# Sums of weight quarters for a Strassen-like product: made in DRAM on one queue, for three more feature tiles, and loaded ready-made

## The chip, the cores and the metric

The kernel runs on one core of a Trainium2 chip. The core has a matrix engine (TensorE; PE in the profile, with its weight loads as PEld), a vector engine (VectorE, DVE), an activation engine (ScalarE, ACT), a general engine (GpSimd, POOL) and a sync engine (SyncE, SP), which in this kernel only issues transfers. Each works through its own list of instructions in order and waits on semaphores; transfers run on 16 DMA engines that all queues share. [...]

The metric is the device time of one execution in microseconds (us): 1148.0 us before the change, the median of three runs (1146.92 to 1148.77).

## The reference

One layer on a sequence of 1024 tokens and a width of 1024, all in float32:

```python
h = x
hn = rmsnorm(h, norm_mix_g)
z = hn @ w_in                                    # pooling columns, then q, k, v of 8 heads
a = pool_mixer(u, pool_w, pool_b, pool_scale)    # trailing means over 2, 4, 8, 16 tokens
o = chunk_attention(q, k, v, rel_bias)           # own chunk of 64 and 8 before, bias per head
h = h + concat([a, o]) @ w_out
hn = rmsnorm(h, norm_ffn_g)
gt, val = split(hn @ w_up)                       # 2 x 2816 columns: "the first projection"
gt = causal_dwconv(gt, conv_w, conv_b)
h = h + (gelu(gt) * val) @ w_down                # "the second projection"
gate = sigmoid(rmsnorm(h, norm_ple_g) @ w_ple_gate + b_ple_gate)
h = h + gate * (p @ w_ple)
return rmsnorm(h, final_g)
```

## The kernel before

Every float32 factor is split into a high and a low part in the matrix engine's format (`split`, L133 to L135: ACT makes the high part at L134, DVE the low part at L135), and each product is three matmuls (`mm3`, L127 to L131). The order of PE's work is written out by hand. The other engines' instructions are put into their lists by a scheduler, which goes by the program's order and by priorities; what the code marks with `keep_in_program_order` stays in the program's order on its queue.

**Stages by time.** To 44 us the first loads, to 284 us attention together with the input projections and the pooling, to 345 us the output projection begins, to about 800 us the rest of it and the first projection, to 1040 us the second projection, then the gate and the end.

**Attention** (the loop over i, L566 to L601) has 64 iterations: 8 heads of 8 token tiles. An iteration computes the scores of tile i (`scores`: PE at L341, L342 or L349, L350, then DVE at L343 or L351, which also adds the head's bias, then ACT's exponential at L353), transposes the probabilities of tile i - 2 (`probs_t`: PE L367, evicted by ACT L374 and DVE L375), and, every second iteration, multiplies two tiles' probabilities with the values (`values(w)`, w = (i - 5) / 2, PE L384 and L385); its output is written to `o32` by DVE at L391. PE's time in between is filled with matmuls of the input projections, whose weights SP loads at L181 into two buffers.

**The bias.** At the first tile of head h, `load_bias(h + 1)` loads the next head's bias (SP, L320) into the buffer that head h - 1 used, so the transfer is issued when that head's last scores are done. ACT negates it (L321), and POOL masks two corners (L322, L323). ACT meets L321 early in the head and stands there until the load has landed; the bias itself is needed a head later.

**The Strassen-like products.** Both projections into and out of the 2816 features use seven products of 2x2 blocks in place of eight. A weight tile has four quarters a11, a12, a21, a22, and the products need a11, a12, a22 and four sums: s1 = a21 + a22 (product 5), s2 = s1 + a11 (6), s4 = s2 + a12 (3), s3 = a21 + a11 (7).

- For the second projection, the sums of its 11 weight tiles k are made in DRAM (`SD`) during attention: `weight_sums(k, part)` in six parts, two iterations apart, with a new k every four iterations from i = 8. SP makes the plain copies (L547: s1 = a21, s3 = a21, s2 = s1, s4 = s2), POOL the accumulates (L550). A part waits for the transfer of the part before it, on whichever queue it stands.
- For the first projection, a feature tile fi from 3 on gets its four quarters by plain loads (L735, SP), and POOL sums them in SBUF (L744). For fi = 0, 1 and 2 (`by_load`) the sums are made by the transfers themselves: `fetch` loads a quarter on SP (L735) and adds a second one with an accumulate of POOL (L737) for products 5 and 7; products 6 and 3 take the buffer of product 5, to which `prepare` adds one more quarter (POOL, L772) after the split of the former value. That is 15 plain loads and 12 accumulates of 256 KB.

`prepare(upto)` splits the weights of the steps up to four ahead of PE, and `fetch` asks for loads up to two steps ahead of that. There are five buffers (`rawu`). `step(fi, n)` runs product n and evicts it; `keep` (L829, L830) is the eviction by ACT that the next product on the same PSUM bank waits for.

**The pooling.** POOL computes the trailing means of groups 2 and 3 (L455 to L469) when their projections are done, late in attention.

## Time and profile before

| what | value |
|---|---|
| runs | 1148.77, 1146.92, 1148.0 us; median 1148.0 us |
| profiled execution | 1149.12 us, its span 1147.3 us |
| PE busy, 0 to 44 us | 40.97 of 44 us |
| 44 to 284 us (attention) | 235.65 of 240 us, DMA share 0.59 |
| 284 to 345 us | 61.00 of 61 us |
| 345 to 800 us (to the end of the first projection) | 452.08 of 455 us, DMA share 0.27 |
| 800 to 1040 us (second projection) | 238.47 of 240 us, DMA share 0.48 |
| 1040 to 1147 us | 97.06 of 107 us |

The profile is one execution; its times are counted from the start of its span. A busy PE is one with a matmul in flight: neighbours overlap, so a stretch can read 100% and still hold the same matmuls in more or less time. A row of the timeline gives start, duration, engine, line, operation, count and, in brackets, the idle time before it with what ended it. "SPq" is SP's list of issues; a transfer's landing is counted from its issue. Where an engine's idle time is put down to a matmul or to an operation that was long done, the wait was for something else, often a transfer.

### The profile page before, as it was taken

Reading aid. Unit: us, or ns where it says so; the run is one execution under the profiler, and the core shown is the slowest. Engines: PE = TensorE matmul, PEld = TensorE weight load, DVE = VectorE, ACT = ScalarE, POOL = GpSimd, SP = SyncE. Lnnn points to the kernel's source line nnn. Section 1 sums busy time; section 2 is a strip of 40 time slices with the busy share of each in tenths; the row PEclk is TensorE's granted clock in tenths of the full one; section 3 lists DMA queues with packets and bytes.
Section 4 is the critical chain, followed back from the end, with each engine's and each line's share of the span. In section 5 each row is a group of like instructions: output and inputs, shape, how many; then the busy total and the mean of one; then the engine's idle time right before and its main releaser. Section 6 shows DMA issues by size and latency. Waiting matters only on the chain.

```text
span 1147.3 us, 15673 instructions
## 1 busy us (share of the span) xinstructions
PE 1125.2 (98%) x5697; PEld 954.8 (83%) x5697; DVE 894.4 (78%) x1396; ACT 582.9 (51%) x1019; POOL 247.4 (22%) x224
## 2 busy tenths in 40 slices
PE   8999989999999999999999999999999999999996
PEld 7988988888888787888888888888788888888996
DVE  7678877878756787998989998898896779774553
ACT  8568677765654544434343434343444557563342
POOL 0012222165003212434343434343000000000000
PEclk9999999999999999999999999999999999999998
DMA  7236788633611163221323131323673564310111
GB/s 264 74 101 143 178 206 187 157 65 123 207 19 28 32 151 100 67 100 66 101 65 110 59 102 61 111 62 121 222 275 101 165 205 162 102 47 1 40 60 49
DMA packets 62701, 128.76 MB, mean 112 GB/s; under 512 B 7360, under 2 KB 9664, under 8 KB 62272
## 3 DMA queue, kind: packets, MB, share of 16 engines
q1 hardware_dynamic: 54416, 113.02, 30.1%
q0 software_dynamic: 8064, 14.68, 8.2%
q8 instruction: 44, 0.72, 0.3%
q14 instruction: 33, 0.27, 0.1%
q10 hardware_dynamic: 144, 0.07, 0.0%
HBM read 112.01 MB, written 38.80 MB: 131 GB/s over the span
## 4 chain that ended last, share of the span: by engine, by line
PE 87%; DVE 4%; issue 3%; DMA 3%; ACT 2%; SPq 0%; DVEq 0%; POOLq 0%; POOL 0%; ACTq 0%
PE PS L129 27%; PE PS L131 27%; PE PS L130 27%; PE PS L367 2%; PE PS L384 1%; PE PS L385 1%; DMA F<-in_w_down 1%; DVE R L135 1%; DVE B L375 1%; DMA F<-in_bias 1%; PE PS L342 1%; PE PS L341 1%; DVE F L343 1%; DMA F<-in_w_qk 1%; ACT F L353 0%
## 5 line engine op out<-in xcount | busy, mean ns | idle before, releaser
L129 PE MATMUL PS<-R,R 128*128 128x512 f32 (+1 forms) x944 | 361.8, 383 | 3.0 <-ACT V L830 1.8
L131 PE MATMUL PS<-R,R 128*128 128x512 f32 (+1 forms) x944 | 358.5, 380 | 0.0
L130 PE MATMUL PS<-R,R 128*128 128x512 f32 (+1 forms) x880 | 340.5, 387 | 0.3 <-DVE R L230 0.3
L135 DVE TENSOR_TENSOR R<-F,R 128x512 fp32r<-128x512 f32 (+1 forms) x214 | 193.5, 911 | 28.5 <-ACT R L134 28.0
L134 ACT ACTIVATE R<-F 128x512 fp32r<-128x512 f32 (+1 forms) x218 | 132.4, 621 | 150.1 <-PE PS L130 83.3
L129 PEld LDWEIGHTS PS<-R,R 128*128 128x128 f32 x944 | 177.7, 188 | 34.9 <-ACT V L830 2.2
L131 PEld LDWEIGHTS PS<-R,R 128*128 128x128 f32 x944 | 177.7, 188 | 33.9 <-DVE R L135 0.4
L130 PEld LDWEIGHTS PS<-R,R 128*128 128x128 f32 x880 | 165.7, 188 | 32.6 <-DVE R L230 1.6
L744 POOL TENSOR_TENSOR F<-F 128x512 f32<-128x512 f32 x76 | 142.7, 1878 | 222.5 <-DVE R L135 142.0
L130 PE MATMUL PS<-B 128*128 128x512 f32 x316 | 123.3, 390 | 1.5 <-DVE B L135 1.5
L129 PE MATMUL PS<-B 128*128 128x512 f32 x316 | 123.4, 390 | 0.0
L131 PE MATMUL PS<-B 128*128 128x512 f32 x316 | 123.1, 390 | 0.0
L134 ACT ACTIVATE B<-F 128x512 fp32r<-128x512 f32 (+1 forms) x86 | 55.8, 649 | 83.3 <-PE PS L130 59.0
L135 DVE TENSOR_TENSOR B<-F,B 128x512 fp32r<-128x512 f32 (+1 forms) x86 | 61.4, 715 | 29.1 <-ACT B L134 28.6
L654 POOL TENSOR_TENSOR small<-small 128x4 f32<-128x4 f32 (+1 forms) x7 | 7.7, 1095 | 338.5 <-DVE small L653 338.5
L130 PE MATMUL PS<-B,R 128*128 128x256 f32 x256 | 72.3, 283 | 0.0
L130 PEld LDWEIGHTS PS<-B 128*128 128x128 f32 x316 | 59.3, 188 | 14.6 <-DVE B L135 2.3
L129 PEld LDWEIGHTS PS<-B 128*128 128x128 f32 x316 | 59.3, 188 | 12.6 <-ACT B L134 0.3
L131 PEld LDWEIGHTS PS<-B 128*128 128x128 f32 x316 | 59.3, 188 | 12.3
L353 ACT ACTIVATE F<-F,small 128x640 f32<-128x640 f32 (+2 forms) x64 | 44.4, 694 | 20.8 <-DVE small L351 12.8
L129 PE MATMUL PS<-B,R 128*128 128x256 f32 x192 | 54.8, 285 | 0.0
L131 PE MATMUL PS<-B,R 128*128 128x256 f32 x192 | 54.5, 284 | 0.0
(163 smaller groups left out, 1934.6 us busy)
## 6 DMA issues: line engine op xcount, KB each, us to landing
F<-in_w_up SPq DMA_DIRECT2D x91, 256.0 KB, 2.8
SD<-in_w_down POOLq DMA_DIRECT2D x44, 256.0 KB, 6.3
GD<-F SPq DMA_DIRECT2D x22, 512.0 KB, 2.6
R<-GD SPq DMA_DIRECT2D x44, 256.0 KB, 5.3
F<-SD SPq DMA_DIRECT2D x44, 256.0 KB, 2.7
F<-in_w_down SPq DMA_DIRECT2D x33, 256.0 KB, 3.5
SD<-in_w_down SPq DMA_DIRECT2D x22, 256.0 KB, 5.3
SD<-SD SPq DMA_DIRECT2D x22, 256.0 KB, 5.0
```

What stands on the lines that cost most here:

```text
L129: pe.matmul(ps, ahi, bhi, start=first, stop=False, skip_group_check=more)
L130: pe.matmul(ps, ahi, blo, start=False, stop=False, skip_group_check=more)
L131: pe.matmul(ps, alo, bhi, start=False, stop=last, skip_group_check=more)
L134: act.activation(hi, src, AF.Copy)
L135: dve.tensor_tensor(lo, src, rv(hi), ALU.subtract)
L341: pe.matmul(PS[:, 4 + z, 0:320], q, K2[:, ks], start=True, stop=False)
L342: pe.matmul(PS[:, 4 + z, 0:320], q, K1[:, ks], start=False, stop=True)
L343: dve.tensor_tensor_reduce(S.rearrange("p (a b) -> p a b", a=2), PS[:, 4:6, 0:320], b.rearrange("p (a b) -> p a b", a=2), 1.0, BIG, ALU.ad ...
L353: act.activation(S[:, 0:n], S[:, 0:n], AF.Exp, bias=s_[:, 0:1], scale=-1.0, accum_out=s_[:, 1:2])
L367: pe.transpose(pst[:, j * P:(j + 1) * P], S[:, j * P:(j + 1) * P], ident)
L375: dve.tensor_tensor(lo, pst, rv(hi), ALU.subtract)
L744: pool.tensor_tensor(rawu[to], rawu[a], rawu[b], op)
```

## The change

The sums move altogether to POOL's queue. `weight_sums` now makes the plain copies there too, and it makes the sums of 14 weight tiles: those of the first projection's feature tiles 0, 1 and 2 come first (`UP_SUMS` = 3), then the 11 of the second projection. A new tile starts every three iterations from i = 7. In each iteration in which parts are due, `sums_due` first lets POOL copy one column of `o32`, the attention output w = (i - 6) // 2, into an unused column of `small`; so the transfers behind it in POOL's list start only when that output has been written. The up projection's tiles 0, 1 and 2 then load their seven factors ready-made, one plain load each on SP, 21 in all; their accumulates are gone.

```diff
+        UP_SUMS = 3
+        SD = [dr.tile([NF // 2 + UP_SUMS, P, 512], F32, name=f"SD{n}") for n in range(4)]
...
-            def copy(t, src):
-                tc.keep_in_program_order(sp.dma_start(t, src))
-            def grow(t, i, j):
-                tc.keep_in_program_order(pool.dma_start(t, weight(k, i, j), accum_op=ALU.add))
-            if part == 0:
-                copy(s1, weight(k, 2, 1))
-                copy(s3, weight(k, 2, 1))
-            elif part == 1:
-                grow(s1, 2, 2)
-                grow(s3, 1, 1)
...
+        def weight_sums(u, part):
+            s1, s2, s4, s3 = [t[u] for t in SD]
+            a11, a12, a21, a22 = [quarter(u, (i, j)) if u < UP_SUMS else weight(u - UP_SUMS, i + 1, j + 1)
+                                  for i in range(2) for j in range(2)]
+            todo = {0: ((s1, a21, None), (s3, a21, None)), 1: ((s1, a22, ALU.add), (s3, a11, ALU.add)),
+                    2: ((s2, s1, None),), 3: ((s2, a11, ALU.add),), 4: ((s4, s2, None),), 5: ((s4, a12, ALU.add),)}
+            for to, src, op in todo[part]:
+                tc.keep_in_program_order(pool.dma_start(to, src, **({"accum_op": op} if op else {})))
+        def sums_due(i, wi):
+            due = [divmod(i - 7 - 2 * part, 3) + (part,) for part in range(6)]
+            due = [(u, part) for u, z, part in due if z == 0 and 0 <= u < NK + UP_SUMS]
+            if due:
+                h, w = wi // 4, wi % 4
+                a = slice(HD * (h % 2), HD * (h % 2) + HD)
+                tc.keep_in_program_order(pool.tensor_copy(small[a, 78:79], o32[a, h // 2, w * 256:w * 256 + 1]))
+            for u, part in due:
+                weight_sums(u, part)
...
-            for part in range(6):
-                k, z = divmod(i - 8 - 2 * part, 4)
-                if z == 0 and 0 <= k < NK:
-                    weight_sums(k, part)
+            if i >= 7:
+                sums_due(i, (i - 6) // 2)
...
-                sp.dma_start(rawu[i], quarter(fi, qs[0]))
-                for q in qs[1:]:
-                    pool.dma_start(rawu[i], quarter(fi, q), accum_op=ALU.add)
-                held[owner, qs[0]] = i
+                if fi in by_load:
+                    src = SD[SUM_OF[q]][fi] if q in SUM_OF else quarter(fi, plain[q])
+                else:
+                    src = quarter(fi, q)
+                sp.dma_start(rawu[i], src)
+                held[owner, q] = i
...
-                if fi in by_load and n in grows:
-                    pool.dma_start(rawu[t], quarter(fi, grows[n]), accum_op=ALU.add)
```

How this stands in the engines' lists, at three places. In the rows, SD0 to SD3 are s1, s2, s4 and s3, F and small are SBUF tiles, and the names behind "waits" are semaphores: DMAHW of SP's transfers, DMASW of POOL's, the others of engines. Line numbers of the changed kernel are one or two off those of before.

SP's list around the bias load that was issued at 154.75 us, before:

```order
L181 DMA F_70<-in_w_in 128x1024 [waits DMAHW7_49,DVE_49,Activation_49]
L547 DMA SD1_77<-SD0_76 16x4096 [waits DMAHW0_49,DMASW5_49]
L547 DMA SD0_76<-in_w_down 128x512 [waits DMAHW1_49]
L547 DMA SD2_78<-SD1_77 16x4096 [waits DMAHW2_49,DMASW7_49]
L547 DMA SD0_76<-in_w_down 128x512 [waits DMAHW3_49]
L547 DMA SD3_79<-in_w_down 128x512 [waits DMAHW4_49]
L547 DMA SD1_77<-SD0_76 16x4096 [waits DMAHW5_49,DMASW1_49]
L547 DMA SD3_79<-in_w_down 128x512 [waits DMAHW6_49]
L547 DMA SD2_78<-SD1_77 16x4096 [waits DMAHW7_49,DMASW3_49]
L181 DMA F_70<-in_w_in 128x1024 [waits DMAHW0_49,DVE_49,Activation_49]
L547 DMA SD0_76<-in_w_down 128x512 [waits DMAHW1_49]
L320 DMA F_70<-in_bias 128x640 [waits DMAHW3_49,DVE_49,Pool_49]
```

and now, from the bias load before it to the one after:

```order
L321 DMA F_70<-in_bias 128x640 [waits DMAHW3_49,DVE_49,Pool_49]
L182 DMA F_70<-in_w_in 128x1024 [waits DMAHW7_49,DVE_49,Activation_49]
L182 DMA F_70<-in_w_in 128x1024 [waits DMAHW1_49,DVE_49,Activation_49]
L321 DMA F_70<-in_bias 128x640 [waits DVE_49,Pool_49]
L182 DMA F_70<-in_w_in 128x1024 [waits DMAHW4_49,DVE_49,Activation_49]
L182 DMA F_70<-in_w_in 128x1024 [waits DMAHW5_49,DMAHW0_49,DVE_49]
L321 DMA F_70<-in_bias 128x640 [waits DVE_49,Pool_49]
```

The sums have left SP's list, and with them SP's waits for POOL's transfers (DMASW) ahead of weight and bias loads.

POOL's list in a head of attention, before:

```order
L322 MEMSET F_70 64x64 [waits DVE_49,Activation_49]
L323 MEMSET F_70 64x64 [waits Pool_49]
L550 DMA SD0_76<-in_w_down 128x512 [waits DMAHW3_49,DMASW5_49]
L550 DMA SD3_79<-in_w_down 128x512 [waits DMAHW4_49,DMASW6_49]
L550 DMA SD1_77<-in_w_down 128x512 [waits DMAHW5_49,DMASW7_49]
L550 DMA SD2_78<-in_w_down 128x512 [waits DMAHW7_49,DMASW0_49]
L550 DMA SD0_76<-in_w_down 128x512 [waits DMAHW4_49,DMASW1_49]
```

and now, around the masks of one head:

```order
L563 COPY small_73<-F_70 64x1 [waits DVE_49,Pool_49]
L554 DMA SD0_76<-in_w_down 128x512 [waits DMASW0_49]
L554 DMA SD3_79<-in_w_down 128x512
L554 DMA SD1_77<-in_w_up 128x512 [waits DMASW4_49]
L323 MEMSET F_70 64x64 [waits Activation_49]
L324 MEMSET F_70 64x64
L563 COPY small_73<-F_70 64x1 [waits Pool_49]
L554 DMA SD1_77<-SD0_76 16x4096 [waits DMASW5_49]
L554 DMA SD2_78<-in_w_up 128x512 [waits DMASW7_49]
```

Each group of transfers now stands behind a copy that waits for an attention output, the plain copies stand among the accumulates, and the masks stand behind the first groups of their head instead of ahead of all.

POOL's list where the first projection begins, before:

```order
L654 TENSOR_TENSOR small_73<-small_73 128x4 [waits DVE_49]
L772 DMA F_70<-in_w_up 128x512 [waits DMASW7_49,DMASW0_49,DVE_49]
L737 DMA F_70<-in_w_up 128x512 [waits DMAHW2_49,DMASW1_49,DVE_49]
L772 DMA F_70<-in_w_up 128x512 [waits DMASW6_49,DMASW2_49,DVE_49]
L772 DMA F_70<-in_w_up 128x512 [waits DMASW3_49,DMASW2_49,DVE_49]
L737 DMA F_70<-in_w_up 128x512 [waits DMAHW7_49,DMASW4_49,DVE_49]
L737 DMA F_70<-in_w_up 128x512 [waits DMAHW0_49,DVE_49]
L772 DMA F_70<-in_w_up 128x512 [waits DMASW4_49,DVE_49]
L772 DMA F_70<-in_w_up 128x512 [waits DMASW6_49,DVE_49]
L744 TENSOR_TENSOR F_70<-F_70 128x512 [waits DMAHW6_49,DMAHW4_49,DVE_49]
```

and now:

```order
L812 TENSOR_TENSOR TB_3184<-TB_3184 128x512 [waits DVE_49]
L653 TENSOR_TENSOR small_73<-small_73 128x4 [waits DVE_49]
L741 TENSOR_TENSOR F_70<-F_70 128x512 [waits DMAHW4_49,DMAHW6_49,DMAHW0_49,DVE_49]
L741 TENSOR_TENSOR F_70<-F_70 128x512 [waits DMAHW5_49,DMAHW2_49,DVE_49]
L741 TENSOR_TENSOR F_70<-F_70 128x512 [waits DMAHW1_49,Pool_49]
```

The accumulates in place are gone; POOL's next work is the sums in SBUF for feature tile 3.

More of the change, by code (lines that the diff above doesn't have):

```diff
@@ L106, in trunk @@
         GD = dr.tile([NF, P, SEQ], F32, name="GD")
-        SD = [dr.tile([NF // 2, P, 512], F32, name=f"SD{n}") for n in range(4)]
+        UP_SUMS = 3
+        SD = [dr.tile([NF // 2 + UP_SUMS, P, 512], F32, name=f"SD{n}") for n in range(4)]
         b_pool = tc.tile_pool(name="b1", bufs=1)
@@ L540, in weight, with quarter @@
             return w_down[k + NK * (j - 1), :, (i - 1) * 512:i * 512]
-        def weight_sums(k, part):
-            s1, s2, s4, s3 = [t[k] for t in SD]
-            def copy(t, src):
-                tc.keep_in_program_order(sp.dma_start(t, src))
-            def grow(t, i, j):
-                tc.keep_in_program_order(pool.dma_start(t, weight(k, i, j), accum_op=ALU.add))
-            if part == 0:
-                copy(s1, weight(k, 2, 1))
-                copy(s3, weight(k, 2, 1))
-            elif part == 1:
-                grow(s1, 2, 2)
-                grow(s3, 1, 1)
-            elif part == 2:
-                copy(s2, s1)
-            elif part == 3:
-                grow(s2, 1, 1)
-            elif part == 4:
-                copy(s4, s2)
-            else:
-                grow(s4, 1, 2)
+        def quarter(fi, q):
+            return w_up[fi, q[0], :, q[1] * 512:(q[1] + 1) * 512]
+        def weight_sums(u, part):
[15 more added lines that the diff above has]
+                weight_sums(u, part)
         load_bias(0)
         for i in range(NI + 3):
-            for part in range(6):
-                k, z = divmod(i - 8 - 2 * part, 4)
-                if z == 0 and 0 <= k < NK:
-                    weight_sums(k, part)
+            if i >= 7:
+                sums_due(i, (i - 6) // 2)
             if i < NI:
@@ L707, in trunk @@
         order = ahead + [(fi, n) for fi in range(NF) for n in steps[fi]]
-        by_load = (0, 1, 2)
-        chains = {1: ((0, 0),), 5: ((1, 0), (1, 1)), 2: ((0, 1),), 7: ((1, 0), (0, 0)), 4: ((1, 1),)}
-        grows = {5: (0, 0), 6: (0, 1)}
+        by_load = range(UP_SUMS)
+        plain = {1: (0, 0), 2: (0, 1), 4: (1, 1)}
+        SUM_OF = {5: 0, 6: 1, 3: 2, 7: 3}
         loads = []
@@ L715, in trunk @@
             if fi in by_load:
-                if n in chains:
-                    loads.append((i, (fi, n), chains[n]))
+                loads.append((i, (fi, n), n))
             else:
                 need = {1: ((0, 0),), 5: ((1, 0), (1, 1)), 2: ((0, 1),), 6: ((0, 0),), 3: ((0, 1),), 7: (), 4: ()}[n]
-                loads += [(i, fi, (q,)) for q in need if not any(l[1:] == (fi, (q,)) for l in loads)]
+                loads += [(i, fi, q) for q in need if not any(l[1:] == (fi, q) for l in loads)]
         prepared, fetched, done = [0], [0], [0]
@@ L727, in fetch @@
             while fetched[0] < len(loads) and not used[fetched[0] % len(rawu)]:
-                place, owner, qs = loads[fetched[0]]
+                place, owner, q = loads[fetched[0]]
                 fi = owner if isinstance(owner, int) else owner[0]
@@ L734, in fetch @@
                 used[i] = True
-                sp.dma_start(rawu[i], quarter(fi, qs[0]))
-                for q in qs[1:]:
-                    pool.dma_start(rawu[i], quarter(fi, q), accum_op=ALU.add)
-                held[owner, qs[0]] = i
-        def quarter(fi, q):
-            return w_up[fi, q[0], :, q[1] * 512:(q[1] + 1) * 512]
+                if fi in by_load:
[4 more added lines that the diff above has]
+                held[owner, q] = i
         def summed(to, a, b, op=ALU.add):
@@ L753, in prepare @@
                 if fi in by_load:
-                    m = n if n in chains else 5
-                    t = held[(fi, m), chains[m][0]]
-                    done_with = [] if n in grows else [t]
+                    t = held[(fi, n), n]
+                    done_with = [t]
                 else:
@@ L922, in weight_sum @@
         def weight_sum(n, k):
-            return SD[{5: 0, 6: 1, 3: 2, 7: 3}[n]][k]
+            return SD[SUM_OF[n]][UP_SUMS + k]
         def T(k):
```

## The prediction

> **What bounds the kernel now.** The page comes first: TensorE (PE) is busy for 98% of the span.

> ```profile
> span 1147.3 us, 15673 instructions
> PE 1125.2 (98%) x5697; PEld 954.8 (83%) x5697; DVE 894.4 (78%) x1396; ACT 582.9 (51%) x1019; POOL 247.4 (22%) x224
> ...
> q0 software_dynamic: 8064, 14.68, 8.2%
> ```

> The change adds no matrix product and takes none away, so only PE's idle time and new stalls can move the end. Next, the busy time in three stretches (us from the start, then length, busy time of PE, PEld, DVE, ACT, POOL, granted clock, DMA share, GB/s): attention, the first projection's first features, and a stretch of its later ones.

> ```profile
> 94.00:236.00 142.00, 137.65 (x893) 122.72 (x893) 113.44 (x276) 103.92 (x223) 32.28 (x48) 1.00 0.74 169
> 370.00:460.00 90.00, 87.08 (x392) 71.51 (x391) 69.57 (x91) 41.51 (x66) 21.19 (x19) 1.00 0.38 93
> 460.00:520.00 60.00, 60.00 (x266) 49.69 (x266) 54.47 (x57) 24.71 (x35) 23.79 (x13) 1.00 0.24 81
> ```

> PE idles 142.00 - 137.65 = 4.35 us in the first and 2.92 us in the second. These 7.3 us, 0.6% of the span, are all that the change can win. The waits of PE name the causes (total us, times, longest):

> ```profile
> PE PS L367 <- DVE B L375: 4.2, 3, 2.9
> PE PS L129 <- ACT V L830: 1.8, 1, 1.8
> ...
> PE PS L129 <- ACT F L830: 1.2, 1, 1.2
> ```

> **Part 1, the first projection.** The timeline (start us, us, engine, line, operation, count, idle before it) of both L830 waits, then the landings of L772's transfers and of SP's plain loads:

> ```profile
> 393.72 0.93 POOL L772 DMA_DIRECT2D F<-in_w_up  x1 [0.95 <-DVE R L135]
> 397.88 1.15 ACT L134 ACTIVATE R<-F 128x512 fp32r<-128x512 f32 x2 [5.30 <-PE PS L131]
> 399.56 0.50 PE L129 MATMUL PS<-R,R 128*128 128x512 f32 x1 [1.75 <-ACT V L830]
> ...
> 429.81 0.63 ACT L134 ACTIVATE R<-F 128x512 fp32r<-128x512 f32 x1 [3.50 <-PE PS L131]
> 430.98 0.50 PE L129 MATMUL PS<-R 128*128 128x512 f32 x1 [1.17 <-ACT F L830]
> ```

> ```profile
> DMA to landing us min/median/max: 3.9/4.1/4.6
> ...
> F<-in_w_up SPq DMA_DIRECT2D x91, 256.0 KB, 2.8
> ```

> An accumulate may start only when the split of the buffer's former value is done, and it lands 4.1 us later (393.72 + 4.1 = 397.8). ACT stands at the next split (5.30 and 3.50 us), and the eviction L830 that PE needs stands behind that. The change takes out all 12 accumulates and makes 21 plain loads out of 15. Each is asked for three steps ahead and waits only for a free buffer. Three steps are 36 matmuls of 60.00 / 266 = 0.23 us, 8.1 us; a load that lands in 2.8 us, or in twice that, is hidden. Six more issues on SP, each below the 0.52 us of the issues shown further down, lie beside some 60 us of products: nothing, and without that cover 3 us. Gain: 1.75 + 1.17 = **2.9 us**, bounded by 0 (another wait right behind) and by 3.5 (each gap also costs the overlap of two matmuls, 0.50 - 0.23). I take 2.9, since the third stretch, where nothing accumulates in place, shows no gap.

> **Part 2, the sums on POOL.** In attention 88 transfers for 11 sums become 112 for 14, all on POOL. Rows of the DMA line, of POOL's pooling and of the attention outputs 0, 23 and 25:

> ```profile
> L550 POOL DMA_DIRECT2D SD<-in_w_down x44 | 37.3, 962 | 42.2 <-issue 30.2 <-DMA SD<-SD 8.9 <-DVE R L277 1.8
> ```

> ```profile
> 236.74 2.69 POOL L455 TENSOR_TENSOR F<-F 128x271 f32<-128x271 f32 x3 [15.88 <-DVE small L354]
> ```

> ```profile
> 72.36 0.41 DVE L391 TENSOR_TENSOR F<-PS,F 64x256 f32<-64x256 f32 x1
> ...
> 231.68 0.43 DVE L391 TENSOR_TENSOR F<-PS,F 64x256 f32<-64x256 f32 x1
> ...
> 243.83 0.41 DVE L391 TENSOR_TENSOR F<-PS,F 64x256 f32<-64x256 f32 x1
> ```

> Output 0 releases the first transfers, output 25 the last: 171 us for 112 issues of 0.96 us. The DMA engines are fuller than POOL. q0 carried 56 accumulates, 0.082 x 1147 / 56 = 1.68 us of all 16 engines for each; the first stretch has a DMA share of 0.74, and if all of that were sums, 14/11 gives 0.94. The queue nearly fills but holds. POOL may fall some us behind in the middle; from iteration 46 on no sum starts, and it recovers. Behind it wait the bias masks L322, which have a head's length, and the pooling of groups 2 and 3: output 23 releases the last transfers ahead of it at 232 us, 5 us before it starts, and POOL had idled 15.88 us for it. The 50 one-column copies have no row; from nothing up to the 0.96 us of an issue for each they add at most 48 us to 112 x 0.96 = 108 us of issues in 171, so even that fits. Nearest are POOL's masks of 64x64, 0.18 us, some 9 us in all; hidden, I take nothing.

> ```profile
> L323 POOL MEMSET F<- 64x64 f32 x8 | 1.5, 182 | 0.4
> ```

> **Part 3, the bias loads.** PE's longest wait is a bias load's. SP's issues, then ACT, then PE, in the order of the wait:

> ```profile
> 102.65 0.33 SPq L320 DMA_DIRECT2D F<-in_bias  x1
> ...
> 152.92 0.52 SPq L181 DMA_DIRECT2D F<-in_w_in  x1
> 153.50 1.14 SPq L547 DMA_DIRECT2D SD<-in_w_down  x2
> 154.75 0.52 SPq L320 DMA_DIRECT2D F<-in_bias  x1
> ```

> ```profile
> 105.83 0.74 ACT L321 ACTIVATE F<-F 128x640 f32<-128x640 f32 x1
> ...
> 131.64 0.74 ACT L321 ACTIVATE F<-F 128x640 f32<-128x640 f32 x1 [0.75 <-DMA F<-in_bias]
> ...
> 161.30 0.74 ACT L321 ACTIVATE F<-F 128x640 f32<-128x640 f32 x1 [2.34 <-DMA F<-in_bias]
> ...
> 188.38 0.74 ACT L321 ACTIVATE F<-F 128x640 f32<-128x640 f32 x1 [1.46 <-DMA F<-in_bias]
> ```

> ```profile
> 163.54 0.77 PE L367 MATMUL PS<-ident,F 128*128 128x128 f32 x5 [2.87 <-DVE B L375]
> ```

> ```profile
> DMA to landing us min/median/max: 3.0/3.2/6.5
> ```

> ```profile
> SPq L547 <- DMA SD<-in_w_down: 105.0, 22, 10.3
> ```

> The load of 154.75 us had a 512 KB weight load and two plain copies ahead of it on SP's queue, took 6.5 us, and ACT waited 2.34 us at L321, PE 2.87. SP itself had stood at L547 (105 us in all). With the sums off SP the weight load can go earlier, the copies are gone, and at 4.4 us of landing the bias is there at 159 us, just as ACT asks (161.30 - 2.34). Gain 2.87 us.

> There is a price. Before, the masks stood in POOL's order ahead of the next accumulates, so the accumulates paused around each bias load. Now they run through it: output 4, which releases some, comes 3.5 us before the issue at 102.65. How long a bias load then takes, no row shows. The nearest is a weight load amid accumulates, at 134.31 us, against the best of its kind:

> ```profile
> F<-in_w_in SPq DMA_DIRECT2D x1, 512.0 KB, 5.7
> ```

> ```profile
> DMA to landing us min/median/max: 3.5/4.2/7.3
> ```

> ```profile
> 99.14 0.43 DVE L391 TENSOR_TENSOR F<-PS,F 64x256 f32<-64x256 f32 x1
> ```

> ```profile
> 108.01 0.82 DVE L375 TENSOR_TENSOR B<-PS,B 128x640 fp32r<-128x640 f32 x1
> ```

> ```profile
> 108.89 0.77 PE L367 MATMUL PS<-ident,F 128*128 128x128 f32 x5
> ```

> Those 2.2 us are for 512 KB; a bias of 320 KB takes 5/8 of it, 1.4: landing L = 4.4 us, bounds 3.0 (nothing added) and 7.3 (the longest of this queue). The load at 102.65 had 3.2 us until ACT asked, and PE had no slack behind it (108.89 against 108.83); the one behind 131.64 was already waited for at about 3.1. So these two turns lose L - 3.2 = 1.2 and L - 3.1 = 1.3 us. The turn at 161.30 wins 2.87 up to L = 4.8 (it issues 0.6 us sooner, without the two copies); that at 188.38, whose load took 4.2, stays. Sum of attention: 1.2 + 1.3 - 2.9 = **-0.4 us**; -4.1 at 3.0 and +11 at 7.3.

> [...]

> **Sum.** -2.9 - 0.4 = -3.3 us. The profiled execution took 1149.1 us, 1.8 of it around its span, and becomes 1145.8; the median of 1148.0 lies 1.1 below it, so the forecast is **1144.7 us**, 0.29% faster. About 0.2%, 2.3 us, is what a measurement of this kernel can tell from no change.

> **The rivals.** (a) The bias loads hardly feel the accumulates (L = 3.0): attention wins 4.1, the sum is -7.0, 1141.0. For it: only the 6.5 us load had much ahead of it. Against: a DMA share near 0.9.

> (b) *Slower*: the accumulates never pause and the bias loads are late at every head. With the four turns above the sum is 4L - 21 us: nothing at L = 5.3, slower by more than 0.2% from L = 5.9, and at 6.5, the longest seen for a bias, +5, 1153. For it: one load did take 6.5, and a weight load 7.3. Against: both had transfers of their own queue ahead, which now leave it.

> (c) It doesn't do what it says: the gaps at 399.56 and 430.98 close, but the next split or eviction holds PE there (DVE is busy 69.57 of 90 us), or L near 5.2 takes the gain back: within 0.2%, about 1148. Against: the later features, with as many splits and a busier DVE, show no gap.

> (d) The copies or a full DMA ring make POOL late by more than the 5 us before the pooling; the mixer's splits follow, and PE waits some 5 us net, 1153. Against: the 15.88 us of idle there.

> **Chances.** Forecast with its neighbours (1143.5 to 1145.7) 0.35, (a) 0.20, (c) 0.26, (b) 0.15, (d) 0.04. Faster 0.55, same 0.26, slower 0.19. Leaving out a tenth on either side, the range is 1140.8 to 1152.5; the faster cases alone fill 1140.8 to 1145.7.

> **What would show it.** Right: no L830 wait of PE before 460 us, no gap of over 1 us near 160 us, waits of ACT at L321 of 1 to 2 us at several heads, a DMA share near 0.9 from 94 to 236 us. Wrong: bias landings of 6 us or more, waits of PE at L367 of over 2 us at several heads, or a pooling that starts after 245 us.

## The result, and the profile after

| | before | after |
|---|---|---|
| median of seven runs on one chip | 1148.77 us | 1158.74 us |
| lowest and highest | 1146.65, 1153.72 us | 1156.72, 1169.40 us |
| ratio | | 1.0091, 95% interval 1.0069 to 1.0114 |

The change makes the kernel 10 us slower, beyond the 0.2% that can be told from nothing and beyond the range on record. The profiled execution of after is the longest of the seven (1169.4 us), so its losses are larger than the usual ones; e1's profile below, of an execution of usual length, shows losses of the same kind.

The page of after, to be held against the first fence of the prediction:

```profile
span 1167.6 us, 15724 instructions
PE 1133.2 (97%) x5697; PEld 963.6 (83%) x5697; DVE 893.8 (77%) x1396; ACT 583.1 (50%) x1019; POOL 287.5 (25%) x328
```

The three stretches of before, in after (length, busy time of PE, PEld, DVE, ACT, POOL, granted clock, DMA share, GB/s):

```profile
94.00:236.00 142.00, 125.67 (x786) 113.46 (x785) 98.79 (x238) 89.44 (x191) 75.45 (x140) 0.94 0.90 206
370.00:460.00 90.00, 90.00 (x410) 74.76 (x410) 66.02 (x92) 45.44 (x74) 15.50 (x11) 1.00 0.22 71
460.00:520.00 60.00, 60.00 (x267) 49.67 (x266) 52.67 (x57) 23.68 (x34) 21.61 (x12) 1.00 0.26 84
```

The second row is part 1 as forecast: the 2.92 us of idle time are gone. The first row is the loss: 16.33 us of idle time where 4.35 stood, a clock of 0.94, and a DMA share of 0.90.

ACT's wait for the five bias loads issued between 90 and 250 us (total us, times; before: 4.6, 3), their landing (before: 3.0/3.3/6.5), and then ACT's rows behind them:

```profile
  ACT F L322: 22.1, 5
...
DMA to landing us min/median/max: 6.7/7.8/8.2
```

```profile
109.71 0.74 ACT L322 ACTIVATE F<-F 128x640 f32<-128x640 f32 x1 [3.59 <-DMA F<-in_bias]
140.55 0.74 ACT L322 ACTIVATE F<-F 128x640 f32<-128x640 f32 x1 [5.89 <-DMA F<-in_bias]
172.58 0.74 ACT L322 ACTIVATE F<-F 128x640 f32<-128x640 f32 x1 [2.86 <-DMA F<-in_bias]
205.11 0.74 ACT L322 ACTIVATE F<-F 128x640 f32<-128x640 f32 x1 [5.41 <-DMA F<-in_bias]
238.08 0.74 ACT L322 ACTIVATE F<-F 128x640 f32<-128x640 f32 x1 [4.38 <-DMA F<-in_bias]
```

and PE's gaps, one behind each of them, in the timeline of PE:

```profile
112.66 0.76 PE L368 MATMUL PS<-ident,F 128*128 128x128 f32 x5 [3.56 <-DVE B L376]
142.51 0.58 PE L131 MATMUL PS<-B,R 128*128 128x256 f32 x1 [4.38 <-DVE B L136]
174.82 0.77 PE L368 MATMUL PS<-ident,F 128*128 128x128 f32 x5 [3.41 <-DVE B L376]
207.49 1.33 PE L368 MATMUL PS<-ident,F 128*128 128x128 f32 x5 [4.87 <-DVE B L376]
245.42 1.33 PE L368 MATMUL PS<-ident,F 128*128 128x128 f32 x5 [4.07 <-DVE B L376]
```

Read the two together: every late bias holds ACT for 3 to 6 us, and 2 to 3 us after ACT's negation has begun (at the last turn 7, with 5 us of held-up work of ACT in between) PE comes out of a gap of 3.4 to 4.9 us, 20.3 us in all. PE's rows name DVE, but DVE had waited 3.53, 3.29 and 5.92 us for ACT's part of the same eviction (L375) at three of them, and 4.46 us for ACT's exponential (L354) ahead of the split at 142.51; both stand behind L322 in ACT's list.

A second loss shows in the granted clock. The 8 us behind four of the gaps, in pieces of 4 us (length, busy time of PE, clock, DMA share, GB/s):

```profile
142.51:146.51 4.00, 4.00 (x18) 0.50 1.00 209
146.51:150.51 4.00, 4.00 (x29) 0.78 1.04 367
...
207.49:211.49 4.00, 4.00 (x16) 0.50 0.95 172
211.49:215.49 4.00, 4.00 (x19) 0.79 0.26 46
245.42:249.42 4.00, 4.00 (x16) 0.50 0.07 29
249.42:253.42 4.00, 4.00 (x20) 0.84 0.02 4
```

Behind three of the gaps PE runs at half clock for 5 to 6 us: each of these stretches loses about 4 x 0.50 + 4 x 0.2 = 2.8 us, and the one behind 174.82 some 1.7 (0.60 and 0.98); behind 112.66 the clock stays at 1.00. The sum for this execution: idle time from 94 to 284 us 20.8 instead of 4.35 (+16.4), half clock +10.0, part 1 -2.9, and 1.5 us less idle time between 460 and 840 us: +22, beside 1167.6 - 1147.3 = 20.3 seen. It closes to 2 us.

### The profile page after: what moved, and what is told of

Same layout as the page of the kernel before. It is cut to its first block, busy times and chain, and to the rows that moved or that the text cites. A ratio compares the mean times of both kernels' runs of the same rounds, so it can differ in the third digit from the quotient of the medians.

```text
span 1167.6 us, 15724 instructions
## 1 busy us (share of the span) xinstructions
PE 1133.2 (97%) x5697; PEld 963.6 (83%) x5697; DVE 893.8 (77%) x1396; ACT 583.1 (50%) x1019; POOL 287.5 (25%) x328
## 4 chain that ended last, share of the span: by engine, by line
PE 87%; DMA 5%; issue 3%; DVE 2%; ACT 2%; POOL 0%; SPq 0%; DVEq 0%; POOLq 0%; ACTq 0%
PE PS L131 27%; PE PS L132 27%; PE PS L130 27%; DMA F<-in_bias 3%; PE PS L368 2%; PE PS L385 1%; PE PS L386 1%; DVE B L376 1%; DVE F L344 1%; DMA F<-in_w_qk 1%; PE PS L343 1%; DMA SD<-SD 1%; PE PS L342 1%; DMA R<-GD 0%; ACT F L354 0%
## 5 line engine op out<-in xcount | busy, mean ns | idle before, releaser
L131 PE MATMUL PS<-R,R 128*128 128x512 f32 (+1 forms) x880 | 341.0, 387 | 0.4 <-DVE R L231 0.3
L136 DVE TENSOR_TENSOR R<-F,R 128x512 fp32r<-128x512 f32 (+1 forms) x214 | 191.5, 901 | 19.4 <-ACT R L135 18.8
L135 ACT ACTIVATE R<-F 128x512 fp32r<-128x512 f32 (+1 forms) x218 | 132.9, 620 | 144.5 <-PE PS L131 86.6
L131 PEld LDWEIGHTS PS<-R,R 128*128 128x128 f32 x880 | 166.0, 189 | 32.5 <-DVE R L231 1.4
L131 PE MATMUL PS<-B 128*128 128x512 f32 x316 | 123.1, 390 | 0.2 <-DVE B L136 0.2
L135 ACT ACTIVATE B<-F 128x512 fp32r<-128x512 f32 (+1 forms) x86 | 55.7, 648 | 79.8 <-PE PS L131 54.5
L136 DVE TENSOR_TENSOR B<-F,B 128x512 fp32r<-128x512 f32 (+1 forms) x86 | 61.2, 713 | 27.7 <-ACT B L135 27.4
L131 PE MATMUL PS<-B,R 128*128 128x256 f32 x256 | 73.0, 285 | 4.4 <-DVE B L136 4.4
L131 PEld LDWEIGHTS PS<-B 128*128 128x128 f32 x316 | 59.3, 188 | 13.1 <-DVE B L136 0.6
L130 PEld LDWEIGHTS PS<-B 128*128 128x128 f32 x316 | 59.3, 188 | 12.2
L554 POOL DMA_DIRECT2D SD<-in_w_down x66 | 52.9, 845 | 36.1 <-issue 24.5
L376 DVE TENSOR_TENSOR B<-PS,B 128x640 fp32r<-128x640 f32 (+2 forms) x64 | 42.0, 656 | 21.2 <-ACT B L375 20.5
L354 ACT ACTIVATE F<-F,small 128x640 f32<-128x640 f32 (+2 forms) x64 | 44.3, 693 | 21.0 <-DVE small L352 12.9
## 6 DMA issues: line engine op xcount, KB each, us to landing
F<-in_w_up SPq DMA_DIRECT2D x85, 256.0 KB, 2.8
SD<-in_w_down POOLq DMA_DIRECT2D x66, 256.0 KB, 5.9
F<-SD SPq DMA_DIRECT2D x56, 256.0 KB, 2.7
GD<-F SPq DMA_DIRECT2D x22, 512.0 KB, 2.6
R<-GD SPq DMA_DIRECT2D x44, 256.0 KB, 5.4
F<-in_w_down SPq DMA_DIRECT2D x33, 256.0 KB, 3.2
SD<-SD POOLq DMA_DIRECT2D x28, 256.0 KB, 5.9
F<-in_w_in SPq DMA_DIRECT2D x10, 512.0 KB, 5.9
```

The source lines that it names most:

```text
L130: pe.matmul(ps, ahi, bhi, start=first, stop=False, skip_group_check=more)
L131: pe.matmul(ps, ahi, blo, start=False, stop=False, skip_group_check=more)
L135: act.activation(hi, src, AF.Copy)
L136: dve.tensor_tensor(lo, src, rv(hi), ALU.subtract)
L354: act.activation(S[:, 0:n], S[:, 0:n], AF.Exp, bias=s_[:, 0:1], scale=-1.0, accum_out=s_[:, 1:2])
L376: dve.tensor_tensor(lo, pst, rv(hi), ALU.subtract)
```

## The experiments

Medians are from runs beside the kernel before on the same chip; the ratio is to that kernel.

| run | median, us | ratio (95%) | idle PE, 94 to 284 us |
|---|---|---|---|
| before (with e1 to e4; e5 to e8; e9 to e11) | 1148.9; 1149.4; 1149.0 | | 4.35 |
| after | 1158.7 | 1.0091 (1.0069 to 1.0114) | 20.8 |
| e4 no sums in attention | 1138.6 | 0.9903 (0.9875 to 0.9930) | 1.1 |
| e1 negation moved in the text only | 1161.1 | 1.0098 (1.0065 to 1.0131) | 13.9 |
| e5 negation late | 1146.9 | 0.9980 (0.9968 to 0.9992) | 3.9 |
| e8 before, negation late | 1144.9 | 0.9969 (0.9957 to 0.9980) | 1.3 |
| e2 before, copies on POOL | 1154.1 | 1.0046 (1.0028 to 1.0063) | 5.7 |
| e3 after, copies on SP | 1185.7 | 1.0310 (1.0285 to 1.0336) | 38.8 |
| e6 after without gates | 1155.4 | 1.0059 (1.0035 to 1.0083) | 15.1 |
| e7 13 sums, pace 4 | 1167.3 | 1.0164 (1.0147 to 1.0181) | 12.2 |
| e9 e5 without gates | 1145.6 | 0.9964 (0.9943 to 0.9985) | 1.6 |
| e10 e9 with 13 sums | 1140.9 | 0.9926 (0.9902 to 0.9950) | 1.2 |
| e11 e5 with copies on SP | 1139.0 | 0.9915 (0.9893 to 0.9938) | 1.3 |

**Is it the transfers at all? e4.**

```diff
-                weight_sums(u, part)
+                if part < 0:
+                    weight_sums(u, part)
...
-                    src = SD[SUM_OF[q]][fi] if q in SUM_OF else quarter(fi, plain[q])
+                    src = quarter(fi, plain.get(q, (1, 0)))
...
-            return SD[SUM_OF[n]][UP_SUMS + k]
+            return weight(k, 1, 1)
```

> The changed kernel without any transfer of the sums in attention (the one-column copies stay); where a sum would be loaded, a plain weight tile of the same size is, so the output is not the reference's. Every theory in which those transfers cost expects bias landings of 2.5 to 3.2 us, no PE idle of over 2 us in attention, granted clock 0.995 or more and 1141 to 1145. If the one-column copies, the other loads or the chip's clock are to blame, the time stays above 1150.

Measured 1138.6 us, a little under the expectation. The stretch of attention, and the row of the bias loads among the DMA issues (count, size, median landing):

```profile
94.00:284.00 190.00, 188.88 (x1186) 167.38 (x1185) 155.58 (x365) 132.37 (x278) 44.74 (x102) 1.00 0.17 54
```

```profile
F<-in_bias SPq DMA_DIRECT2D x8, 320.0 KB, 2.9
```

So the sums' transfers cost 20 us in after, and 10 in before, whose twelve accumulates in place are also gone here. The one-column copies, which stay in e4, cost nothing that shows (PE idles 1.1 us in the stretch).

**Is it ACT's stand? e1, e5, e8.** e1 put the negation of the bias five tiles later in the program:

```diff
-            act.activation(b, b, AF.Copy, scale=-1.0)
+        def negate_bias(h):
+            b = biasb[h % 2]
+            act.activation(b, b, AF.Copy, scale=-1.0)
...
+                if t == 4 and h + 1 < N_HEADS:
+                    negate_bias(h + 1)
```

> The changed kernel, with the negation of each head's bias (ACT) and its two masks (POOL) moved from the load to the fifth tile of the head before, some 13 us behind the load; the first head keeps its place. Theory A (ACT standing in order at the negation behind a load of 7 to 8 us is what costs): no wait of ACT at the negation over 1 us although the loads still land after 6 us or more, PE waits at L368's line (the identity product that opens a score's transposes) under 4 us in sum instead of 16.3, granted clock back at 0.99 or more, time 1143 to 1148. Rival B (the full DMA rings as such, through late weight loads and starved splits): a gain of under 4 us, time 1154 to 1159, PE idle elsewhere in attention.

Measured 1161.1 us. The edit didn't do what it says: the scheduler gave the negation the same places in ACT's list from the second head on, so it still stands right behind the load, and the run is nearly a repeat of after, in an execution of usual length:

```profile
107.48 0.74 ACT L324 ACTIVATE F<-F 128x640 f32<-128x640 f32 x1 [3.11 <-DMA F<-in_bias]
...
197.02 0.74 ACT L324 ACTIVATE F<-F 128x640 f32<-128x640 f32 x1 [4.76 <-DMA F<-in_bias]
```

It says nothing for or against either theory. e5 ties the place down by data: the factor -1 is worked out from a value of the fifth tile.

```diff
+                dve.tensor_scalar(minus, after, 0.0, -1.0, ALU.mult, ALU.add)
+            act.activation(b, b, AF.Copy, scale=-1.0 if after is None else minus)
...
+                if t == 4 and h + 1 < N_HEADS:
+                    negate_bias(h + 1, st[i % 3][:, 2:3])
```

> The changed kernel, with the negation of each next head's bias tied by data to a value of the fifth tile (its factor -1 is worked out from that tile's softmax column), so that it can't stand right behind the load: some 13 us later on ACT, its masks on POOL behind it. Theory A (the stand of ACT at the negation is the way by which the full DMA rings hold PE, and each hold of some 3 us brings a stretch at half clock behind it): no wait of ACT at the negation over 0.5 us, no gap of PE over 2 us between 94 and 284 us, clock 0.994 or more, 1141 to 1147 although the sums' transfers and the landings stay as in the change. Rival B (weight loads that land late, and POOL late, hold PE just as well): 1150 to 1158.

Measured 1146.9 us, at the upper edge of theory A's range: 12 us of after's time gone. The bias landings from 90 to 250 us, the attention row, and the waits of PE in that stretch (total us, times, longest):

```profile
DMA to landing us min/median/max: 4.3/7.0/7.5
```

```profile
94.00:284.00 190.00, 186.13 (x1169) 164.14 (x1168) 149.41 (x360) 131.03 (x274) 112.24 (x208) 1.00 0.83 190
```

```profile
PE PS L373 <- DVE B L381: 2.6, 4, 1.7
```

The loads land as late as ever (7.0 us against 7.8) with the DMA engines fuller (0.83 against 0.79 in the same stretch of after), and PE no longer minds: none of ACT's waits in this stretch is for a bias load, where after's were 22.1 us. This is the main result: the late landing costs through ACT's place in line, not by itself. Late weight loads (median landing 5.7 us in e5, 5.9 in after) were no cause: with ACT free the gap of 142.51 us behind a weight split went too.

> The kernel before with the late negation of e5. Theory A: its three waits of PE behind the negation (4.2 us in sum) go, no others come: 1143 to 1146. Rival B: nothing, 1147 to 1150, or slower, since POOL's masks, and with them the accumulates behind them, go out some 13 us later in each head.

e8, the same edit on the kernel before, gave 1144.9 us, 4.5 us faster than before. Its bias landings rose to 6.1 us at the median (4.9 to 7.4), since POOL's masks no longer hold the accumulates back around the load, and PE's idle time in attention fell all the same, to 1.3 us.

**Which part made the loads late? e2, e6, e7, e3.** e2 is the queue move alone, at the old pace:

```diff
             def copy(t, src):
-                tc.keep_in_program_order(sp.dma_start(t, src))
+                tc.keep_in_program_order(pool.dma_start(t, src))
```

> The kernel before, with one edit: the plain copies of the 11 sums go out on POOL's queue instead of SP's; pace (a sum begins every 4 tiles), gates and the first projection as before. Theory A says the pace of 3 tiles and the gates behind attention outputs keep accumulates running through the bias loads, so here POOL still stands at the masks around each load: bias landings of 3 to 4.5 us at the median, time 1144 to 1149. Rival C (the queue that the copies use is what does it: SP's weight and bias loads now run beside copies they used to follow): landings of 6 us or more, time 1154 or more.

Measured 1154.1 us, between the two. The landings from 90 to 250 us are in between as well, and one gap now brings a half clock where before's longest, 2.87 us, brought none:

```profile
DMA to landing us min/median/max: 2.9/4.7/6.5
```

```profile
192.08 1.07 PE L367 MATMUL PS<-ident,F 128*128 128x128 f32 x5 [3.24 <-DVE B L375]
```

```profile
192.00:196.00 4.00, 3.92 (x17) 0.57 0.94 144
```

So the queue alone brings 5 of the 13 us that after loses outside part 1. In the profiled execution they add up: 1.35 us more idle time in attention and two half clocks of 1.7 us each, this one and one at 403.51 us, give 4.75 of the 4.9 us between the two spans. But the second half clock stands behind a gap of part 1, which before has too, so how much of the 5 us is the bias loads' isn't settled.

e6 takes out the gates behind attention outputs:

```diff
-                tc.keep_in_program_order(pool.tensor_copy(small[a, 78:79], o32[a, h // 2, w * 256:w * 256 + 1]))
```

> The changed kernel without the one-column copies: the sums of the 14 tiles go out as early as POOL's own order lets them, only the bias masks hold POOL. If the gates behind attention outputs are what puts accumulates beside the bias loads, POOL stands at the masks again, bias landings fall to 3 to 5 us and the time to 1144 to 1150. If 14 sums in 171 us fill the rings whatever their pacing, the landings stay at 6 us or more and the time at 1154 to 1162.

Measured 1155.4 us, landings 5.9 to 7.6 us: the second case. By the medians the gates are worth some 3 us, but the intervals of after and e6 overlap, so that isn't clear of noise; the loads land late without gates too.

e7 lowers the pace, with 13 sums:

```diff
-        UP_SUMS = 3
+        UP_SUMS = 2
...
-            due = [divmod(i - 7 - 2 * part, 3) + (part,) for part in range(6)]
+            due = [divmod(i - 7 - 2 * part, 4) + (part,) for part in range(6)]
```

> The changed kernel with 13 sums (two feature tiles of the first projection by sums instead of three; the third by quarter loads and vector work as the other 19) and a sum begun every 4 tiles instead of 3, gates kept: the same traffic a tile as before the change, all on POOL. If the pace is what costs, DMA share falls to 0.75 and bias landings to 3 to 4.5 us, and the time to 1146 to 1150. If gates and queue cost at any pace, 1153 to 1158.

Measured 1167.3 us, worse than either case. Attention alone did gain (12.2 us idle, not 20.8; DMA share 0.73 there), though its bias loads landed in 6.4 us at the median and not in 3 to 4.5, so the pace alone isn't what makes them late. And at this pace the sums last until 300 us, and their issues lie between the poolings of the same engine. DVE, then PE:

```profile
293.60 0.44 DVE L456 TENSOR_TENSOR F<-F 128x271 f32<-128x271 f32 x1 [9.41 <-POOL F L456]
```

```profile
295.29 0.58 PE L386 MATMUL PS<-B,R 128*128 128x256 f32 x1 [5.32 <-DVE B L376]
```

That is rival (d) of the prediction, by a path that it didn't name: DVE has to wait for a scratch tile that POOL's pooling holds.

e3 puts the copies back on SP and leaves the rest:

```diff
-                tc.keep_in_program_order(pool.dma_start(to, src, **({"accum_op": op} if op else {})))
+                tc.keep_in_program_order(pool.dma_start(to, src, accum_op=op) if op else sp.dma_start(to, src))
```

> The changed kernel with the plain copies of the sums back on SP's queue; 14 sums, pace 3, gates and accumulates on POOL as in the change. Theory A: the bias loads stand behind copies on SP's queue and still beside accumulates: landings of 6 us or more, time 1155 to 1165. Rival C: landings of 3 to 4.5 us, time 1144 to 1149.

Measured 1185.7 us, 20 beyond the worse case. SP stands at copies that wait for accumulates, the bias load is issued late behind them, and ACT waits 13 us:

```profile
SPq L554 <- DMA SD<-in_w_down: 115.7, 20, 14.7
```

```profile
222.66 0.74 ACT L322 ACTIVATE F<-F 128x640 f32<-128x640 f32 x1 [13.02 <-DMA F<-in_bias]
```

So at the new pace the move to POOL's queue spares 27 us; with ACT standing, that pace is dear on either queue.

What orders most of these kernels is how long POOL, which issues the accumulates, stands idle just ahead of the masks, around each bias load: 10.6 to 14.4 us in before, 6.4 to 9.2 in e2, 4.7 to 7.9 in e7, 2.1 to 5.0 in e6 and not at all in after, with median landings of 3.3, 4.7, 6.4, 6.4 and 7.8 us. e3, whose copies SP issues, falls out of the order (4.5 to 12.6 us, and 7.8). Only e8 tests the pause by itself: with before's traffic, and the masks moved away from the load, the landing rose from 3.3 to 6.1 us.

**What is best once ACT doesn't stand? e9, e10, e11.**

> e5 (the change with the late negation) without the one-column copies as well, so that the 14 sums go out as early as POOL's order lets them. If what is left in e5 is POOL's late end (its pooling started at 243 us instead of 237, and PE waited 2.8 us at 294.9 us behind it), the pooling starts before 240 us, that gap goes and the time is 1141 to 1145, below both kernels. If the rings are full either way: 1146 to 1150, as e5.

e9 is e5 without the gates' line. Measured 1145.6 us, its runs from 1138.6 to 1149.3; the pooling began at 240.39 us. The gap that was to go is still in its profile:

```profile
292.06 0.50 PE L130 MATMUL PS<-B 128*128 128x512 f32 x1 [2.94 <-ACT B L135]
```

The waits of DVE say how a late pooling gets there. In e9 and in e5 alike, DVE waits once for POOL's scratch tile, as in e7:

```profile
DVE F L461 <- POOL F L461: 4.0, 1, 4.0
```

DVE's splits behind it run late, the load of `pool_w` waits for one of them, and ACT's split that PE waits for stands 4.1 to 4.2 us for that load. In e10 and e11 DVE has no such wait, and ACT stands 1.8 us there.

> e9 with 13 sums instead of 14 (two feature tiles of the first projection by sums, the third by quarter loads and vector work): 8 transfers less. Same reasons as e9; less traffic, so the pooling starts some 8 us sooner than in e9 where the rings set it. 1141 to 1145 if POOL's end is what counts, no more than 1 us from e9 if not.

e10 has `UP_SUMS = 2`. Measured 1140.9 us, its pooling from 236.45 us, no such gap: 4.7 us below e9, so POOL's end does count. (It also has 8 transfers less, and this run can't tell the two apart.)

> e3 (the change with its plain copies back on SP's queue, 1185.7 us) with the late negation. If e3's 27 us over the change come by the same stand of ACT behind bias loads that SP issues late, they go: 1145 to 1150. If they come by late weight loads behind SP's waits for accumulates, most stay: 1160 or more, with PE waiting behind the split of weights (L136's line) and not behind the identity products.

e11 is e5 with e3's line. Measured **1139.0 us**, 0.85% faster than before and within 0.5 us of e4, the kernel that makes no sums. All of e3's loss went with ACT's stand. Its landings, its rows, and the start of its pooling:

```profile
DMA to landing us min/median/max: 6.7/8.0/8.7
```

```profile
94.00:284.00 190.00, 188.73 (x1183) 166.53 (x1182) 156.92 (x370) 132.75 (x278) 85.74 (x157) 1.00 0.83 193
284.00:460.00 176.00, 176.00 (x792) 145.82 (x792) 126.67 (x180) 89.81 (x144) 26.71 (x18) 1.00 0.25 78
```

```profile
234.54 2.06 POOL L461 TENSOR_TENSOR F<-F 128x271 f32<-128x271 f32 x3
```

The bias loads land later than in any other kernel, 8.0 us at the median, and PE has lost 1.3 us in attention and none from there to 460 us. With half of the issues on SP, POOL reaches its pooling 8.6 us before e5 does (243.13 us), and e5's gap there of 2.8 us is gone.

## Why the prediction was wrong, step by step

- **Part 1 was right.** The gaps at 399.56 and 430.98 us are gone in every kernel with the plain loads. Their price can be larger by a half clock: in e8, which keeps them, the gap at 395.75 us, of 1.86 us, is followed by one (0.57 over 4 us).
- **Part 2 was right in the load and wrong in what covers POOL.** The DMA share came out at 0.90 (forecast: up to 0.94). But the 15.88 us that POOL had idled before its pooling were used up: in e5, where PE runs on time, POOL goes straight from an issue into its pooling, 6.4 us later than in before. After's own start, 262.74 us, says less, since POOL had stood 11.49 us shortly before for an attention output that PE's own losses delayed. What the late pooling costs, e5 and e9 show: 5 to 8 us against e10 and e11, whose pooling is early. The one-column copies are 48, not 50.
- **Part 3 failed, in its price.** The step was the landing L beside accumulates that no longer pause, 4.4 us by 5/8 of one weight load's surplus; it was 7.8 us. A term was missing as well: the half clock behind a gap, 10.0 us in the profiled execution, stood in the sum at nothing. The row that the price rested on was a load issued at 134.31 us, just behind the masks for which POOL had stood 10.88 us, when the accumulates had only begun:

```profile
132.44 0.42 POOL L322 MEMSET F<- 64x64 f32 x1 [10.88 <-ACT F L321]
132.91 0.15 POOL L323 MEMSET F<- 64x64 f32 x1
133.02 2.50 POOL L550 DMA_DIRECT2D SD<-in_w_down  x3
```

  In after the engines are nearly full through attention, as in the window of its worst turn (DMA share 0.98, clock 0.89):

```profile
130.00:160.00 30.00, 25.61 (x173) 24.39 (x172) 20.20 (x50) 15.75 (x37) 15.65 (x32) 0.89 0.98 225
```

  The bound of 7.3 us was nearer than the value taken. Before's own bias loads held a better measure, the DMA share from issue to landing; here for the load that took 3.0 us and for the one that took 6.5 (length, busy time of POOL, clock, DMA share, GB/s):

```profile
102.65:105.65 3.00, 0.00 (x0) 1.00 0.39 109
154.75:161.25 6.50, 0.00 (x0) 1.00 0.87 284
```

  The prediction put the 6.5 us down to what stood ahead on SP's queue. In after nothing of the sums stood there, the share was 0.88 or more for all five loads, and they took 6.7 to 8.2 us.
- **The gain at 161.30 us** didn't come: that turn's load (ACT at 172.58 us) was late by 2.86 us like the others.
- **Rival (b) is what happened**, with a chance of 0.15. Its formula gives 4 x 7.8 - 21 = +10.2 us, beside the median's +10.0, but that close a match is luck: it had four turns and no half clock, the trace has five gaps and four stretches at half clock. Its argument against itself, that the slow loads had had transfers of their own queue ahead, didn't hold.
- **The mechanism that it rests on**, ACT's stand at the negation, is shown by e5 and e11: landings as late (7.0 and 8.0 us), hardly a loss. That it takes the sums' transfers as well is shown by e4.
- Of the signs on record, "bias landings of 6 us or more", "waits at L367 of over 2 us at several heads" and "a pooling that starts after 245 us" all came, the last in part through PE's own delay: in e5, with PE on time, the pooling starts at 243.13 us.

Left open: how much of e2's 5 us is the bias loads', and why accumulates that don't pause make a load of 320 KB land in 7.8 us rather than 5 or 10.

## What to carry to other kernels

A transfer needed a whole stage later can still be critical, as the bias loads here: with ACT's stand behind them gone, after's 1158.7 us became 1146.9 (e5). Look for the first instruction that waits for such a transfer, and at what stands behind that on an in-order engine. Such an instruction is best tied to the place where it belongs by data (e5), since moving its line need not move it in a scheduled list (e1, 1161.1 us). And before filling the DMA queues, list each load that now finds them half empty (before's three at a share of 0.39 to 0.40), and price it by its longest landing, not by its median: before's were 6.5 and 3.3 us, and after's median was 7.8.

## What the runs showed of the hardware

```profile
395.75 0.50 PE L129 MATMUL PS<-R,R 128*128 128x512 f32 x1 [1.86 <-ACT V L838]
```

```profile
394.00:396.00 2.00, 0.25 (x1) 1.00 0.00 0
396.00:400.00 4.00, 4.00 (x12) 0.57 0.62 196
400.00:404.00 4.00, 4.00 (x19) 1.00 0.55 78
```

Of the gaps from 1.2 to 1.8 us, seven of them, none was. Which gap is followed, these runs don't tell: before's 2.87 us gap wasn't, nor the one of 2.81 us in e5, while 2.04 us in e7 was (0.57). That fits the spread among executions of one kernel (after: 1156.7 us at a mean clock of 0.993, 1169.4 at 0.984).

**In these runs the landing times of the bias loads went with how full the DMA engines were while the load was under way**, more than with the mean of the stage. From 94 to 236 us the mean share is 0.74 in before, 0.76 in e2, 0.77 in e7 and 0.78 in e8, but the median landings are 3.3, 4.7, 6.4 and 6.1 us. From issue to landing it was 0.39 to 0.40 for before's three loads of 3.0 to 3.3 us, 0.66 to 0.77 for e7's (4.7 to 6.8 us) and 0.88 or more for those of after and e8 (4.9 to 8.2 us). Nor is it what stands ahead in the load's own queue: over all eight bias loads the median is 2.9 us without sums, 3.2 in before, 4.3 with before's copies on POOL and 7.2 in after, while SP's queue ahead of them grew emptier from before to e2 and after.
